# Staging the attention keys: copies by VectorE into three tiles, for transfers into two

## The chip, the cores and the metric

The kernel runs on one core of a Trainium2 chip. The core has five engines that work side by side, each through its own queue in order: TensorE (PE, matmuls and transposes into PSUM), VectorE (DVE), ScalarE (ACT), GpSimd (POOL) and SyncE (SP), which here only issues transfers. The metric is the time of one execution in microseconds on the device. The time before is a median over three runs.

## The reference

Two layers of a transformer trunk work on 512 latent tokens (a grid of 8 rows by 64 columns) and 256 context tokens, with 1024 channels. Each layer normalizes and modulates its input, projects it with one matrix into keys, values, queries and gates, and runs two attentions side by side:

```python
qa = _rmsnorm(hs(a_q, NA_HEADS), q_norm_a)
ka = _rmsnorm(hs(a_k, NA_HEADS), k_norm_a)
a_att = _na_latent(qa, ka, va, cka, cva, rpb, rows)
qb = _rope_2d(_rmsnorm(hs(b_q, GQA_Q_HEADS), q_norm_b), pos_row, pos_col)
b_att = _gqa_latent(qb, k_all, v_all)
out_x = _merge(a_att, b_att, a_z, b_z, g_a, g_b, w_o_a, w_o_b, w_out)
x_new = x + gate_x * out_x
```

The first is neighbourhood attention with 8 heads of 64 channels: a latent query sees a window of 8 rows by 16 columns, with a learned bias, and all context keys. The second is grouped-query attention with 8 query heads and 2 key heads over all 768 tokens. In layer 0 the context tokens are updated too, with queries of their own; layer 1 computes only the latent ones.

## The kernel before, in words

Everything is computed in float32 quality on faster number types. A projection splits weights and activations into a high and a low part and adds three products (`mm3`, lines 460 to 462). Weight chunks are loaded by SP (`load_w2`, line 442, tile `raw`), rounded by ScalarE (line 445, `whi`), and VectorE or GpSimd computes the low part (line 447, `wlo`). Attention works on pairs of fp16 numbers, high and low.

Keys after the turn to channels lie in the tile `ka`, 128 rows by (high or low, four head pairs, 768 tokens). The 128 rows hold the two heads of a pair: the even head in rows 0 to 63, the odd one in rows 64 to 127. The query tile `qa` holds, for one head, the high part in that head's own row half and the low part in the other half. So one matmul over 128 rows forms high and low query times the key, provided the head's 64 key rows stand in both row halves. Making that copy is `stage_k`: for one head it writes a tile of 128 x (2, 768) fp16, twice from the same 64 rows. Before, each half is one transfer issued by SP (line 910). For neighbourhood attention the tile is `akt[e]`, one for the even and one for the odd heads (line 1064), so a head can be staged once the scores of the head two before it are read. For the grouped-query keys `stage_k` fills the tile `gk`, during two of the query projections (lines 1173 to 1175), twice a layer.

The heads go through `pipeline` (line 1045): scores of head h, then values of head h - 1, then a share of a list of independent projections (`fill`, for gates and the other branch), whose matmuls stand between those of the heads. The chain of one head's block of 128 queries is: scores on TensorE (lines 918, 919, 1006), bias and row maximum on VectorE (line 1009), exponential on ScalarE (line 1012), reciprocal and scaling (lines 841 to 847), then `turned`: high half on ScalarE (line 888), low half on GpSimd (line 889), and a transposing transfer issued by SP (line 893) into the tile `ht`. Blocks that are not transposed by transfers go through TensorE and lines 858 to 865. The values are lines 1030 to 1040, and `head_out` (lines 878 to 880) puts them in `za`. SP also issues loads of bias (lines 981 and 983), weights, and stores of gates (line 662).

The order on each engine is written into the program beforehand: a planner walks the listed instructions by their place in the program, with a cost model of its own, and gives each engine its fixed queue. Waits are semaphores. A tile made with a tag and a number of buffers is a ring: the next use of a slot waits until the earlier use has been read.

Of the kernel before, what the change touches and what calls it, by code (L numbers as in the profile page):

```python
# [10 lines left out]
F16 = mybir.dt.float16  # L11
# [63 lines left out]
def hybrid_kernel(es: ExitStack, tc, x, ctx, cvec, w_ada, w_ada0, small, gvec, w_in, w_o_a, w_o_b, w_out,  # L75
                  bias_int, bias_edge, rope, ident_d, out):
    nc = tc.nc
    V, S, G, T = nc.vector, nc.scalar, nc.gpsimd, nc.tensor
# [10 lines left out]
    def nm(s):  # L89
        uid[0] += 1  # L90
        return f"{s}_{uid[0]}"
# [536 lines left out]
    def layer(l, hx, nxt, start):  # L628
# [20 lines left out]
        att = {}  # L649
# [94 lines left out]
        kav = pairs("ka")  # L744
# [93 lines left out]
        if True:  # L838
# [65 lines left out]
            def rows(a, half):  # L904
                return a[64 * half:64 * half + 64]

            def stage_k(src, j, e, to):

                for half in range(2):
                    nc.sync.dma_start(rows(to, half), rows(src, e)[:, :, j, :])  # L910

            def q_pair(src, e, j):
                return src[:, e, j, :]
# [10 lines left out]
            def ctx_scores(q, kh, kl, ct, late=True):  # L924

                pss = ps_score()
                for i in range(2):
                    scores(pss, q[:, 512 + 128 * i:640 + 128 * i], kh, kl,
                           [(256 * i, 256, cut(512, 768))])
                mx = sp.tile([128, 2], F32, tag="mx", name=nm("mx"), bufs=8)  # L930
                V.tensor_reduce(mx, pss.rearrange("p (i n) -> p i n", i=2), AX, ALU.max, negate=True)
                dq = gq_dq if late else na_dq[:, l:l + 1]
                V.tensor_scalar(mx, mx, dq, P_LOG if late else 0.0, ALU.mult, ALU.add)
                p = p_tile()
                r = sp.tile([128, 2], F32, tag="r", name=nm("r"), bufs=8)
                for i in range(2):
                    S.activation(p[:, 256 * i:256 * i + 256], pss[:, 256 * i:256 * i + 256], AF.Exp,
                                 bias=mx[:, i:i + 1], scale=dq, accum_out=r[:, i:i + 1])
                if not late:
                    softmax_tail(p, 512, r, mx, [(0, 256), (256, 512)])  # L940
                turned(p, 512, ct.rearrange("p a i k n -> p (a i k) n"), G)
                return ct, r
# [118 lines left out]
                values_of(7, prev)  # L1061
                run(fill, len(fill))

            akt = [att["p"].tile([128, 2, 768], F16, name=nm("kk"), bufs=1) for _ in range(2)]

            def na_first(h):
                j, e = h // 2, h % 2
                kh, kl = akt[e][:, 0], akt[e][:, 1]
                stage_k(kav, j, e, akt[e])
                q = q_pair(qav, e, j)  # L1070
                st = na_scores(h, q, kh, kl)
                if not first:
                    return st, None
                o = 4096 + 1024 * (h % 2)
                ct = turns[:, o:o + 1024].rearrange("p (a i k n) -> p a i k n", a=2, i=2, k=2)
                return st, ctx_scores(q, kh, kl, ct, False)
# [9 lines left out]

            bg = []
            pipeline(fill, 9, na_first, values_of(za, na_values, vsa[:, 1:2], False), bg=bg)


# [77 lines left out]
            for t in range(qt):  # L1168
                tok_proj(w_q, 512, a_hx, t, evac_bq)
                run(bg, 2)  # L1170
                if t == STAGE_T[0]:
                    split_vb()
                if t in STAGE_T:
                    e = STAGE_T.index(t)
                    stage_k(kbv, 0, e, gkt[:, e])
# [69 lines left out]
        with tc.tile_pool(name=f"mrg{l}", bufs=1, reuse_waits="tile") as mp:  # L1245
# [3 lines left out]
            for v in range(nv):  # L1249
                src = gd[l][8 * v:8 * v + 8].rearrange("k p -> (k p)").unsqueeze(0)  # L1250
# [236 lines left out]
    def nxt():  # L1487
        if not hx1:
            hx1.extend([[big("hx") for _ in range(2)] for _ in range(2)])
        return hx1  # L1490
    layer(0, hx0, nxt, start)
    layer(1, hx1, None, None)


# [73 lines left out]
```

## Time and profile before

| | us |
|---|---|
| median of 3 runs | 1138.68 (1135.82 to 1139.03) |
| the profiled execution | 1141.91 |
| its span in the trace | 1140.0 |
| TensorE busy | 1080.4 |
| VectorE busy | 756.2 |
| ScalarE busy | 608.6 |
| GpSimd busy | 451.1 |

The profiled execution is one run recorded by the hardware; its span starts and ends with the first and last recorded instruction. Rows of groups read: line, engine, operation, output and inputs, shapes, count, then total busy us and mean ns of one, then idle time of the engine before them with what ended it. Rows of waits read: who waited for whom, total us, times, longest. Rows of one line or tile have the shortest, median and longest duration in ns. Rows of a timeline begin with start and duration in us. A line like L447 is a line of the program.

### The profile page before, as it was taken

The numbers are of one execution on the slowest core, as the hardware profiler recorded it, in microseconds if no ns is written. First come the engines' busy times: TensorE is split into PE (matmuls) and PEld (weight loads), VectorE is DVE, ScalarE is ACT, GpSimd is POOL, SyncE is SP. The second block draws the span as 40 slices with busy tenths as digits, with TensorE's granted clock in tenths as the row PEclk, the third lists the DMA queues.
The fourth block names the chain that finished last, engine by engine and source line by source line (L and its number), as shares of the span: only waits on it lengthen the run. The fifth ranks groups of instructions, "written<-read, shape, count | busy, mean of one in ns | idle before, by whom it ended". The sixth has DMA issues, their size and how long they took to land. (4 is left out here: it accounts for less than half of the span.)

```text
span 1140.0 us, 16941 instructions
## 1 busy us (share of the span) xinstructions
PE 1080.4 (95%) x5672; PEld 849.9 (75%) x5672; DVE 756.2 (66%) x1627; ACT 608.6 (53%) x1219; POOL 451.1 (40%) x393
## 2 busy tenths in 40 slices
PE   8999999999999999988999999999987899999998
PEld 5688877788988867665888778887765787666677
DVE  4667978765488577666577775576674675677473
ACT  5455368676333567665230264646685435777431
POOL 1054225455154235374322525332243463564530
PEclk8999999999999999989999999999998999999999
DMA  9555346665553488789433533744566445879742
GB/s 360 199 170 177 90 112 146 155 155 133 176 148 132 122 204 181 162 225 238 158 131 100 188 108 114 232 138 130 121 155 168 131 139 161 194 227 224 199 146 79
DMA packets 249711, 186.08 MB, mean 163 GB/s; under 512 B 160924, under 2 KB 215064, under 8 KB 247960
## 3 DMA queue, kind: packets, MB, share of 16 engines
q1 hardware_dynamic: 242144, 170.47, 55.1%
q0 software_dynamic: 2368, 7.87, 2.1%
q10 hardware_dynamic: 5112, 6.66, 1.9%
q8 instruction: 45, 0.74, 0.3%
q14 instruction: 42, 0.34, 0.1%
HBM read 118.86 MB, written 20.47 MB: 122 GB/s over the span
## 5 line engine op out<-in xcount | busy, mean ns | idle before, releaser
L889 POOL TENSOR_TENSOR h<-p,h 128x256 f16<-128x256 f32 (+2 forms) x104 | 108.5, 1051 | 166.0 <-ACT h L888 127.9
L447 POOL TENSOR_TENSOR wlo<-raw,whi 128x512 fp32r<-128x512 f32 x70 | 96.9, 1387 | 134.6 <-ACT whi L445 108.5
L460 PE MATMUL psf<-hx,whi 128*128 128x512 f32 (+1 forms) x360 | 140.6, 391 | 4.4 <-ACT zt L658 2.2
L462 PE MATMUL psf<-hx,wlo 128*128 128x512 f32 (+1 forms) x360 | 137.9, 383 | 0.0
L461 PE MATMUL psf<-hx,whi 128*128 128x512 f32 (+1 forms) x360 | 137.7, 383 | 0.0
L445 ACT CAST whi<-raw 128x512 fp32r<-128x512 f32 x136 | 83.1, 621 | 79.2 <-DMA raw<-in_w_in_dram 48.7
L461 PE MATMUL psx<-wlo,hx 128*128 128x512 f32 (+1 forms) x328 | 120.8, 369 | 1.3 <-DVE wlo L433 1.3
L460 PE MATMUL psx<-whi,hx 128*128 128x512 f32 (+1 forms) x328 | 121.0, 371 | 0.0
L462 PE MATMUL psx<-whi,hx 128*128 128x512 f32 (+1 forms) x328 | 120.5, 368 | 0.0
L433 POOL TENSOR_TENSOR wlo<-raw,whi 128x512 fp32r<-128x512 f32 x40 | 58.9, 1476 | 125.2 <-ACT whi L430 80.2
L430 ACT CAST whi<-raw 128x512 fp32r<-128x512 f32 x88 | 54.1, 625 | 92.6 <-PE psx L462 31.9
L533 POOL TENSOR_TENSOR ss<-ss,ehalf 128x8 f32<-128x8 f32 (+2 forms) x40 | 63.6, 1595 | 93.0 <-DVE ss L530 88.4
L447 DVE TENSOR_TENSOR wlo<-raw,whi 128x512 fp32r<-128x512 f32 x66 | 70.0, 1063 | 42.2 <-ACT whi L445 41.0
L1199 ACT ACTIVATE p<-pss,mx,vb 128x768 f32<-128x768 f32 x64 | 63.5, 993 | 46.8 <-DVE mx L1198 44.2
L888 ACT CAST h<-p 128x256 f16<-128x256 f32 (+2 forms) x136 | 82.0, 618 | 8.4 <-DMA ht<-h 5.9
L1198 DVE CUSTOM_DVE_ANT_0 p<-pss,vb 128x768 f32<-128x768 f32 x64 | 64.1, 1013 | 28.7 <-PE pss L919 23.9
L460 PEld LDWEIGHTS psf<-hx,whi 128*128 128x128 f32 x360 | 69.4, 193 | 17.6 <-ACT zt L658 3.8
L462 PEld LDWEIGHTS psf<-hx,wlo 128*128 128x128 f32 x360 | 69.1, 192 | 12.3
L461 PEld LDWEIGHTS psf<-hx,whi 128*128 128x128 f32 x360 | 69.2, 192 | 11.2
L460 PE MATMUL psx<-hx,whi 128*128 128x256 f32 (+1 forms) x208 | 70.5, 339 | 6.6 <-ACT whi L445 6.6
L461 PEld LDWEIGHTS psx<-wlo,hx 128*128 128x128 f32 x328 | 62.0, 189 | 12.1 <-DVE wlo L433 2.4
L462 PE MATMUL psx<-hx,wlo 128*128 128x256 f32 (+1 forms) x208 | 69.8, 335 | 0.2 <-POOL wlo L447 0.2
(348 smaller groups left out, 2869.4 us busy)
## 6 DMA issues: line engine op xcount, KB each, us to landing
raw<-in_w_in_dram SPq DMA_DIRECT2D x168, 256.0 KB, 3.1
rawb<-in_w_ada_dram SPq DMA_DIRECT2D x48, 256.0 KB, 2.7
raw<-in_w_out_dram SPq DMA_DIRECT2D x32, 256.0 KB, 3.1
kk<-ka SPq DMA_DIRECT2D x32, 192.0 KB, 3.4
tg<-gs SPq DMA_DIRECT2D x4, 1536.0 KB, 8.2
rawx<-in_w_ada_dram SPq DMA_DIRECT2D x4, 1024.0 KB, 8.5
rawy<-in_w_ada_dram SPq DMA_DIRECT2D x4, 1024.0 KB, 11.1
gs<-zt ACTq DMA_DIRECT2D x16, 256.0 KB, 3.2
```

Of the source, the lines that this page charges most:

```text
L430: S.copy(hi[:, :n], raw[:, :n])
L433: e.tensor_tensor(lo[:, :n], raw[:, :n], F(hi[:, :n]), ALU.subtract)
L445: S.copy(hi, raw)
L447: lo_eng(i).tensor_tensor(lo, raw, F(hi), ALU.subtract)
L460: T.matmul(ps, lhs[0], rhs[0], start=first, stop=False)
L461: T.matmul(ps, lhs[0], rhs[1], start=False, stop=False)
L462: T.matmul(ps, lhs[1], rhs[0], start=False, stop=last)
L533: G.tensor_tensor(ss, ss, ehalf[:, :n], ALU.pow)
L888: S.copy(h[:, 0], p[:, :n])
L889: eng.tensor_tensor(h[:, 1], p[:, :n], h[:, 0], ALU.subtract)
L1198: V.tensor_tensor_reduce(p, pss, lift, gq_ndq, 3e38, ALU.add, ALU.min, mx[:, 0:1])
L1199: S.activation(p, pss, AF.Exp, bias=mx[:, 0:1], scale=gq_dq, accum_out=r[:, i:i + 1])
```

## The change

`stage_k` issues no transfers any more. VectorE copies the 64 rows of the head into both row halves, one instruction for each half. It is used for the neighbourhood keys (8 heads in each of 2 layers, 32 copies) and for the grouped-query keys (2 key heads in each layer, 8 copies). For the neighbourhood keys, the two fixed tiles are replaced by a ring of three tiles that the heads take in turn.

```diff
             def stage_k(src, j, e, to):
 
                 for half in range(2):
-                    nc.sync.dma_start(rows(to, half), rows(src, e)[:, :, j, :])
+                    V.tensor_copy(rows(to, half), rows(src, e)[:, :, j, :])
...
-            akt = [att["p"].tile([128, 2, 768], F16, name=nm("kk"), bufs=1) for _ in range(2)]
-
             def na_first(h):
                 j, e = h // 2, h % 2
-                kh, kl = akt[e][:, 0], akt[e][:, 1]
-                stage_k(kav, j, e, akt[e])
+                kk = att["p"].tile([128, 2, 768], F16, tag="kk", name=nm("kk"), bufs=3)
+                kh, kl = kk[:, 0], kk[:, 1]
+                stage_k(kav, j, e, kk)
```

## The prediction

> **What bounds the kernel now.** I read the page's first lines, then the table of stretches over the stages that stage keys, then what TensorE waited for in them, then the rows of the moved transfers, and last the timeline around the longest stop.
>
> ```profile
> span 1140.0 us, 16941 instructions
> PE 1080.4 (95%) x5672; PEld 849.9 (75%) x5672; DVE 756.2 (66%) x1627; ACT 608.6 (53%) x1219; POOL 451.1 (40%) x393
> ```
>
> TensorE is busy for 1080.4 of 1140.0 us, so all its idle time is 59.6 us. An edit that leaves the matmuls alone can win only out of that, and loses only by adding to it.
>
> ```profile
> core 0: us, PE busy (x) PEld busy (x) DVE busy (x) ACT busy (x) POOL busy (x), PEclk, DMA share, GB/s
> 140.00:290.00 150.00, 144.69 (x882) 117.98 (x881) 106.74 (x311) 102.80 (x237) 67.99 (x75) 0.99 0.59 141
> 780.00:895.00 115.00, 99.99 (x522) 73.33 (x521) 67.78 (x202) 75.58 (x168) 43.13 (x48) 0.97 0.57 141
> 320.00:380.00 60.00, 59.58 (x301) 49.35 (x300) 42.51 (x83) 22.46 (x44) 26.64 (x18) 1.00 0.45 136
> 905.00:945.00 40.00, 38.93 (x193) 32.02 (x192) 30.75 (x57) 16.55 (x37) 24.97 (x21) 1.00 0.45 130
> ```
>
> The first two stretches are the neighbourhood attention of layer 0 and layer 1, the last two hold the staging of the grouped-query keys. TensorE is idle for 5.3 us in the first and 15.0 us in the second. VectorE is busy 71% and 59% of them. What TensorE waited for in layer 0's stretch (first fence) and in layer 1's (second); columns are total us, times, longest:
>
> ```profile
> PE psv L1030 <- DVE ho L879: 2.3, 1, 2.3
> PE psf L460 <- DVE za L660: 2.2, 1, 2.2
> ```
>
> ```profile
> PE psx L460 <- ACT whi L445: 6.6, 2, 6.1
> PE psv L1030 <- DMA ht<-h: 2.0, 2, 1.6
> PE pst L858 <- ACT p L845: 1.8, 2, 1.4
> PE psv L1030 <- ACT h L888: 1.4, 1, 1.4
> PE psv L1030 <- DVE ho L879: 1.4, 1, 1.4
> ```
>
> Most of these end on the softmax chain (row maximum, exponential, scaling, halves, transpose), which runs through VectorE. The 6.1 us stop is another thing: it waits for weights. Its timeline, SP first, then ScalarE, then TensorE:
>
> ```profile
> 842.34 0.66 SPq L910 DMA_DIRECT2D kk<-ka  x1
> ...
> 845.71 0.64 SPq L910 DMA_DIRECT2D kk<-ka  x1
> ...
> 848.27 14.02 SPq L893 DMA_TRANSPOSE ht<-h  x10
> 862.34 0.57 SPq L662 DMA_DIRECT2D gs<-zt  x1
> 863.01 0.94 SPq L442 DMA_DIRECT2D raw<-in_w_in_dram  x2
> ```
>
> ```profile
> 864.63 0.60 ACT L658 ACTIVATE zt<-psf 128x512 f32<-128x512 f32 x1 [2.35 <-DMA gs<-zt]
> 866.26 1.38 ACT L445 CAST whi<-raw 128x512 fp32r<-128x512 f32 x2 [1.03 <-DMA raw<-in_w_in_dram]
> ```
>
> ```profile
> 866.93 0.79 PE L460 MATMUL psx<-hx,whi 128*128 128x512 f32 x1 [6.15 <-ACT whi L445]
> ```
>
> SP spends 14.02 us on ten transposes, and the store and the weight load behind them leave only then. The key copies are part of the same queue.
>
> **The change part by part.** *Removed: 40 transfers from SP.*
>
> ```profile
> L910 SPq DMA_DIRECT2D kk<-ka x32: 607/644/1689, 144.7 to 866.6; - x32
> L910 SPq DMA_DIRECT2D gk<-kb x8: 497/589/609, 335.3 to 927.2; - x8
>   DMA kk<-ka: 0.9, 2
> DMA to landing us min/median/max: 2.7/3.4/4.5
> ```
>
> SP gets back 32 x 0.644 + 8 x 0.589 = 25.3 us. Almost none of it is on the path: TensorE waited for these transfers 0.9 us in all. What the queue gives back elsewhere is bounded by the rows of layer 1 that hang on SP: the weights' 6.6 and the transposes' 2.0, so with the 0.9 at most 9.5 us, and at least nothing. I take the two issues just ahead of the ten transposes, 0.66 + 0.64 = 1.3 us, because a queue that starts them earlier ends them earlier by no more, and the 0.9: **-2.2 us** (0 to -9.5).
>
> *Added: 40 copies on VectorE,* each 64 rows of 2 x 768 fp16. The trace has no copy from fp16 to fp16. The nearest rows have one input in SBUF:
>
> ```profile
> L375 DVE CAST hx<-half 128x512 fp32r<-128x512 f32 x12 | 5.1, 424 | 12.8 <-ACT half L371 12.8
> L385 DVE TENSOR_SCALAR x<-x,ss 128x512 f32<-128x512 f32 x12 | 5.8, 483 | 7.4 <-POOL ss L388 7.4
> L359 DVE TENSOR_SCALAR y<-xt,ss 128x1024 f32<-128x1024 f32 x6 | 4.5, 746 | 0.5 <-POOL ss L357 0.5
> L847 DVE TENSOR_SCALAR_CACHE_REDUCE p<-p,r 128x512 f32<-128x512 f32 x32 | 23.7, 740 | 0.4
> L847 DVE TENSOR_SCALAR_CACHE_REDUCE p<-p,r 128x256 f32<-128x256 f32 x16 | 7.6, 477 | 0.5
> L447 DVE TENSOR_TENSOR wlo<-raw,whi 128x512 fp32r<-128x512 f32 x66 | 70.0, 1063 | 42.2 <-ACT whi L445 41.0 <-PE psf L462 0.8
> ```
>
> L385 to L359 gives (746 - 483) / 512 = 0.514 ns a word; L375 then has 424 - 263 = 161 ns beside its words. A row of a copy holds 3,072 bytes, 768 words: 161 + 0.514 x 768 = 556 ns. The dear end is one element at a time, by L847 (740 - 477) / 256 = 1.03 ns: 161 + 1.03 x 1536 = 1.74 us. The cheap end is L375 itself, 0.42 us. I take 0.56, since an ordinary copy is nearest to L375, a cast, and not to L847, which also sums. To this comes waiting for GpSimd:
>
> ```profile
> L447 DVE TENSOR_TENSOR wlo<-raw,whi x66: 668/694/3998, 99.2 to 1070.6; 128x512 fp32r<-128x512 f32 x66
> L375 DVE CAST hx<-half x12: 413/427/428, 655.6 to 688.5; 128x512 fp32r<-128x512 f32 x12
> ```
>
> L447 has a median of 0.694 and a mean of 1.063 us: 0.37 us a piece lost when it runs beside GpSimd's own L447. L375 shows no such spread. I take the 0.37, so a copy is **0.93 us**, and 40 make 37.2 us: VectorE goes from 756.2 to 793.4 us.
>
> The Trainium skill, "SBUF — State Buffer", section "Who interferes with whom", says that a VectorE copy in a two-port mode and a GpSimd instruction exclude each other for a whole instruction, whichever starts first. By it the copies lose time as L447 does and also hold GpSimd up; L375 alone, which never spread, would say that neither happens. With the lock the sum below is as it stands; without it the copy is 0.56 us, and the forecast would be about 1139.6.
>
> *What of the copies is on the path.* A head takes two, 1.86 us. They stand in VectorE's queue, whose rows, maxima and low halves they delay. In layer 1 six waits of TensorE end on the softmax chain (2 + 2 + 1 + 1 in the rows above); a copy is in front of ready work about as often as VectorE is busy, 59%: 6 x 1.86 x 0.59 = 6.6 us. In layer 0 there are two, 2 x 1.86 x 0.71 = 2.6 us. Against these 9.2 us stands the ring: a third tile lets copies run a head or two early, in VectorE's idle third. I take half, **+4.6 us** (0 to 14.9, which is all eight waits at the full 1.86).
>
> *Cover.* Elsewhere in these stages the copies are hidden by the fill, the projections for gates and values that keep TensorE at 144.69 of 150 us in layer 0; where it runs out, as at 861 us, every head's pair shows, 1.86 us. The eight grouped-query copies (7.4 us) fall where TensorE is busy for 59.58 of 60 and 38.93 of 40 us: **+0.5 us** (0 to 1.5, its idle time there). The wait for a free ring tile moves from SP to VectorE. Behind it stand the next row maxima, and ScalarE waits for those; but the tile was last read three heads earlier, so I put it at 0 (bound: one head's pair, 1.9).
>
> *GpSimd.* It too is stretched at times:
>
> ```profile
> L889 POOL TENSOR_TENSOR h<-p,h x104: 662/679/2380, 162.5 to 1061.9; 128x256 f16<-128x256 f32 x64, 128x768 f16<-128x768 f32 x32, 128x512 f16<-128x512 f32 x8
> ```
>
> Its longest low half takes 2.38 us. If a copy holds it as VectorE is held in L447, its instructions start late: 16 copies x 0.56 us x its busy share, 45% and 38%, is 4.0 and 3.4 us. Half of layer 1's six waits (the transposes' two and the one for L888's halves) lie on the chain that passes GpSimd; half of 3.4 is **+1.7 us** (0 to 7.4). Where layer 1's stop goes, the late thing is next the transposes of the last head.
>
> *The sum.* -2.2 + 4.6 + 0.5 + 1.7 = +4.6 us on the profiled execution, which took 1141.91 us: 1146.5. The median of the three runs, 1138.68, is 3.2 us below it, so I forecast **1143.3 us**. The planner redraws the order of all engines from new costs; the same code idled TensorE for 5.3 us in one layer and 15.0 in the other, so I allow 5 us either way.
>
> **The rivals.** *SP was the brake (faster).* With its copies gone SP reaches the store and the weights of layer 1 early enough that the 6.15 us stop goes, and the transposes' waits with it. For it: SP's unbroken run from 842 to 864. Against it: only 1.3 us of this run are key copies. It gains the 9.5 us; with 2 us lost to the copies, the time is 1138.7 - 7.5 = 1131.2. It decides once SP comes to the load at 863.0 us by over 5 us earlier, more than the copies cost above.
>
> *Hidden both ways (no change).* The ring lets every copy fall into VectorE's idle time (43.3 and 47.2 us) and SP's relief ends in waits for GpSimd. For it: TensorE's 95%. Against it: VectorE's queue is in order, and its idle time is waiting that a ready copy can't always use. Time 1138.7.
>
> *The copy is dear, or not early (much slower).* At 1.74 + 0.37 us, 16 copies are 33.8 us, and layer 0's VectorE would be busy for 140.5 of 150 us; the ring then gains nothing. All eight waits take 2 x 2.11: 8 x 4.22 x 0.6 = 20 us, less 2.2: 1157. The planner setting each pair right before its head's scores, which would make the third tile idle, ends between this and the forecast. Against both: L375.
>
> **How the numbers follow.** Forecast 0.37; SP as the brake 0.33; hidden 0.16; dear or late 0.14. 0.3% of 1138.68 is 3.4 us, about what a measurement of this kernel can tell from no change. Slower is 0.37 + 0.14 = 0.51, same 0.16, faster 0.33. The forecast's own range is 1139 to 1150: the sum's terms with the planner's 5 us. As the signs are split, the range for all runs from the gain of SP less a little, 1130, to the dear copy's near end, 1155.
>
> **What would show it.** Right: copies of about 0.6 us, often stretched to 1 us or more beside GpSimd; VectorE near 793 us; no key transfer on SP; TensorE's waits in layer 1 on ScalarE's and VectorE's softmax lines longer, its idle time there above 15.0 us. Wrong: layer 1's stop before a weight load gone and its stretch shorter than 115 us (SP was the brake), copies at 1.7 us (dear), or TensorE's idle time growing in stages that stage no keys (the planner).

## The result, and the profile after

The changed kernel takes 1130.07 us in the median (1129.48 to 1131.95, 6 runs) against 1138.86 us for the kernel before (1133.20 to 1141.79, 6 runs): a ratio of 0.9933, 95% interval 0.9908 to 0.9958. It is faster by 0.7%, where I had forecast 0.4% slower. First the page of the changed kernel, its head and engines:

```profile
span 1127.7 us, 16945 instructions
PE 1075.9 (95%) x5672; PEld 844.4 (75%) x5672; DVE 786.4 (70%) x1667; ACT 608.8 (54%) x1219; POOL 453.6 (40%) x393
```

The span is 12.3 us shorter, where the medians differ by 8.8: the profiled execution of the kernel before, 1141.91 us, was slower than its median, and that of the changed kernel, 1129.48, the fastest of its six. TensorE is busy for 4.5 us less with the same 5,672 matmuls, and idle for 51.8 us and not 59.6. VectorE has 30.2 us more. Then what has taken the place of the transfers, from the rows of the key tiles and the groups of VectorE:

```profile
L910 DVE COPY kk<-ka x32: 543/558/1616, 152.1 to 835.8; 64x1536 f16<-64x1536 f16 x32
L910 DVE COPY gk<-kb x8: 543/555/558, 338.1 to 914.1; 64x1536 f16<-64x1536 f16 x8
L910 DVE COPY kk<-ka 64x1536 f16<-64x1536 f16 x32 | 26.8, 839 | 0.6
```

A copy takes 0.558 us in the median, with a mean of 0.839 us among the neighbourhood keys and up to 1.616 us. The timeline shows where they stretch, VectorE's pairs of copies first, then GpSimd beside the first of them:

```profile
805.92 2.11 DVE L910 COPY kk<-ka 64x1536 f16<-64x1536 f16 x2
...
824.68 1.11 DVE L910 COPY kk<-ka 64x1536 f16<-64x1536 f16 x2
```

```profile
806.09 1.52 POOL L447 TENSOR_TENSOR wlo<-raw,whi 128x512 fp32r<-128x512 f32 x1 [2.40 <-ACT whi L445]
```

The pair at 824.68 us, with GpSimd idle until 825.94, takes 1.11 us; the one that meets GpSimd's low half takes 2.11. To see where the time went I measure each layer's stage between two landmarks that both kernels have: the first memset of `bint` and the load of `cosn`, with which the next stage begins. The rows of the kernel before, then of the changed one (the second number of each range is layer 1's):

```profile
L975 DVE MEMSET bint<- x2: 272/272/272, 151.3 to 777.4; 128x256 f32 x2
L1099 SPq DMA_DIRECT2D cosn<-in_rope_dram x2: 342/362/383, 289.3 to 893.6; - x2
```

```profile
L975 DVE MEMSET bint<- x2: 272/272/272, 151.2 to 778.0; 128x256 f32 x2
L1098 SPq DMA_DIRECT2D cosn<-in_rope_dram x2: 384/403/422, 289.9 to 878.4; - x2
```

Up to layer 1's stage nothing is won: it begins 0.6 us later. The stage shrinks from 116.2 to 100.4 us, by 15.8; from there to the end 2.9 us are given back. (The load of `cosn` is issued by SP itself, so its place isn't quite the same in both kernels.) The stretch from landmark to landmark, first before, then after:

```profile
777.40:893.60 116.20, 101.19 (x521) 74.06 (x520) 69.29 (x207) 76.40 (x169) 44.42 (x49) 0.97 0.57 141
```

```profile
778.00:878.40 100.40, 93.88 (x489) 67.59 (x488) 82.31 (x223) 75.94 (x170) 45.28 (x49) 1.00 0.51 128
```

TensorE's idle time in it falls from 15.0 to 6.5 us. 32 matmuls are done later instead, which fits with what is given back. What TensorE still waited for (780 to 895 us, changed kernel):

```profile
PE psv L1030 <- DMA ht<-h: 4.1, 1, 4.1
PE pss L1006 <- DVE mx L1009: 2.1, 3, 0.9
```

The 6.1 us stop before a weight load is gone. A new one of 4.1 us stands at the end, before the last head's values, which wait for its transposes; the granted clock behind it is 0.65 from 878.1 to 882.0 us, which lies past the landmark and belongs to what is given back. The old stop cost more than itself, as the stretches around it in the kernel before show (the number behind POOL's is the granted clock):

```profile
860.00:866.00 6.00, 0.47 (x3) 0.20 (x2) 2.01 (x3) 2.83 (x6) 1.93 (x2) 0.95 0.62 168
866.00:873.00 7.00, 6.07 (x16) 4.78 (x17) 1.86 (x2) 2.48 (x4) 2.56 (x2) 0.55 0.95 259
873.00:880.00 7.00, 7.00 (x35) 5.31 (x34) 3.60 (x11) 3.41 (x7) 2.88 (x2) 1.00 0.51 153
```

The granted clock over the 7 us behind the stop is 0.55, with 16 matmuls where the next 7 us hold 35. TensorE is busy for 6.07 of them; 0.45 of that, some 2.7 us by this estimate, is what the low clock adds to the stop. The Trainium skill, "TensorE: Matmul & The Clock Gate", section "HAM oscillation — how this bites in real kernels", says that idle gaps over about 3.4 us put TensorE's clock back to half; this trace agrees with its 0.55 behind 6.15 us. It doesn't agree with 3.4 us as the least: in the kernel before, TensorE also stands idle for 2.34 us until 219.53 us, and from 220.3 to 223.7 us the granted clock is 0.50.

SP's queue in the changed kernel is not empty at all:

```profile
809.58 1.74 SPq L442 DMA_DIRECT2D raw<-in_w_in_dram  x3
...
837.82 6.41 SPq L893 DMA_TRANSPOSE ht<-h  x5
...
846.08 7.73 SPq L893 DMA_TRANSPOSE ht<-h  x6
853.91 1.18 SPq L983 DMA_DIRECT2D bedg<-b_edge  x2
855.19 7.07 SPq L893 DMA_TRANSPOSE ht<-h  x5
...
866.47 1.60 SPq L442 DMA_DIRECT2D raw<-in_w_in_dram  x3
```

Three runs of transposes, of 6.41, 7.73 and 7.07 us, follow each other with little between them, where before 14.02 us stood without a break. But the weights were fetched earlier (809.58 us), so TensorE waits for none here, and the last head's keys are copied at 835 us, where before their transfers left at 865.9.

### The profile page after: what moved, and what is told of

Its sections match the earlier page's. It is cut to its first block, busy times and chain, and to the rows that moved or that the text cites. A ratio compares the mean times of both kernels' runs of the same rounds, so it can differ in the third digit from the quotient of the medians.

```text
span 1127.7 us, 16945 instructions
## 1 busy us (share of the span) xinstructions
PE 1075.9 (95%) x5672; PEld 844.4 (75%) x5672; DVE 786.4 (70%) x1667; ACT 608.8 (54%) x1219; POOL 453.6 (40%) x393
## 5 line engine op out<-in xcount | busy, mean ns | idle before, releaser
L889 POOL TENSOR_TENSOR h<-p,h 128x256 f16<-128x256 f32 (+2 forms) x104 | 110.4, 1068 | 156.4 <-ACT h L888 128.7
L460 PEld LDWEIGHTS psf<-hx,whi 128*128 128x128 f32 x360 | 68.3, 190 | 19.5 <-DVE za L660 4.7
L462 PEld LDWEIGHTS psx<-whi,hx 128*128 128x128 f32 x328 | 61.9, 189 | 10.1 <-DVE hx L376 0.4
```

Source lines behind the costliest of these rows:

```text
L460: T.matmul(ps, lhs[0], rhs[0], start=first, stop=False)
L462: T.matmul(ps, lhs[1], rhs[0], start=False, stop=last)
L889: eng.tensor_tensor(h[:, 1], p[:, :n], h[:, 0], ALU.subtract)
```

## The experiments

Two numbers tell the kernels apart: how long layer 1's stage takes, and when in it the last head's scores begin (both from the first memset). They are from one traced execution of each kernel. Ratios are to the kernel before, run on the same chip.

| kernel | keys by | stage, us | last head at | ratio (95%) |
|---|---|---|---|---|
| before | SP | 116.2 | 97.6 | 1 |
| e8_turned_before | SP | 114.3 | 97.2 | 1.0003 (0.9985 to 1.0021) |
| e5_layer0 | SP in layer 1 | 114.6 | 97.7 | 1.0011 (0.9997 to 1.0026) |
| e12_tied | VectorE, tied to SP | 116.2 | 99.5 | 1.0011 (0.9994 to 1.0028) |
| e1_ring_dma | SP, ring | 107.6 | 87.0 | 0.9958 (0.9935 to 0.9981) |
| e11_early | SP, ring, a head early | 108.0 | 83.0 | 0.9953 (0.9929 to 0.9978) |
| e3_act_queue | ScalarE's queue | 109.0 | 80.5 | 0.9950 (0.9930 to 0.9970) |
| e13_pool_queue | GpSimd's queue | 103.9 | 79.6 | 0.9967 (0.9955 to 0.9980) |
| e15_pool_early | GpSimd's queue, ring, early | 101.9 | 79.0 | 0.9936 (0.9916 to 0.9955) |
| after | VectorE, ring | 100.4 | 72.3 | 0.9933 (0.9908 to 0.9958) |
| e7_turned_after | VectorE, ring | 101.0 | 72.5 | 0.9916 (0.9886 to 0.9946) |
| e4_layer1 | VectorE, ring, in layer 1 | 101.2 | 72.9 | 0.9923 (0.9897 to 0.9948) |
| e2_dve_two | VectorE, two tiles | 102.7 | 76.7 | 0.9897 (0.9871 to 0.9922) |
| e9_sp_dummy | VectorE, two tiles | 102.2 | 79.6 | 0.9915 (0.9887 to 0.9942) |
| e10_sp_tiny | VectorE, two tiles | 99.3 | 76.4 | 0.9857 (0.9828 to 0.9885) |
| e16_tiny64 | VectorE, two tiles | 99.6 | 76.9 | 0.9844 (0.9830 to 0.9859) |
| e14_scratch_copies | VectorE, two tiles | 111.2 | 94.2 | 1.0060 (1.0044 to 1.0076) |
| e6_double | VectorE, ring | 114.0 | 91.5 | 1.0152 (1.0123 to 1.0181) |

Not every row is another order of the work. Compared by operation and tile, the matmuls of layer 1 stand in one order in the kernel before, e8 and e5, and in one order in the changed kernel, e7 and e4; e9, e10 and e16 have one order on all five engines throughout, and e15 differs from e13 only in GpSimd's order and, slightly, in SP's. Rows of one order also tell how well a stage repeats: 114.3 to 116.2 us in the first group, 100.4 to 101.2 in the second.

**Which part, and which layer.** My first theory behind the result was SP's relief: 25 us less to issue. The rivals were the ring and an accident of the planner's order.

e1_ring_dma, the ring with SP's transfers:

```diff
+                kk = att["p"].tile([128, 2, 768], F16, tag="kk", name=nm("kk"), bufs=3)
...
                     nc.sync.dma_start(rows(to, half), rows(src, e)[:, :, j, :])
```

> The ring alone: keys are still copied by transfers on SP, but into the ring of three tiles. Theory SP (the gain of 8.8 us, 1138.9 to 1130.1, is SP's relief in layer 1): no gain, 1136 to 1141. Rival ring (the third tile lets heads be staged early): 1130 to 1133. Rival order (the planner's new order is what gains, whatever the cause it was redrawn for): any time in 1130 to 1145, and a layer 1 stretch that differs from 115 us without SP having less to issue.

1134.46 us, between the theories: some of a gain without any relief of SP. e2_dve_two, the copies with the two fixed tiles:

```diff
-                    nc.sync.dma_start(rows(to, half), rows(src, e)[:, :, j, :])
+                    V.tensor_copy(rows(to, half), rows(src, e)[:, :, j, :])
```

> The copies alone: VectorE copies into the two fixed tiles. Theory SP: all of the gain, 1128 to 1133, TensorE's stop before the weight load in layer 1 gone. Rival ring: little of it, 1136 to 1141, with VectorE waiting for tiles to come free. Rival order: any time in 1128 to 1145.

1125.81 us, below every range given: all of the gain is in the copies, and the third tile isn't needed (the two intervals overlap). e3_act_queue, the transfers on ScalarE's queue:

```diff
-                    nc.sync.dma_start(rows(to, half), rows(src, e)[:, :, j, :])
+                    S.dma_start(rows(to, half), rows(src, e)[:, :, j, :])
```

> The same 40 transfers into the two fixed tiles, issued from ScalarE's queue and not SP's: SP is as free as in the change, the data still moves by the transfer engines, and VectorE has no copies. Theory SP: 1127 to 1134, less what ScalarE loses to 40 issues, 25 us of its queue at 0.63 us each. Rival traffic (the 7.9 MB moved less is what gains): 1136 to 1142. Rival order: any.

1131.74 us, about half of e2's gain, with all the data still moved by transfers: this much needs no less traffic. e4_layer1 and e5_layer0 make the change where `l == 1` and where `l == 0`:

> The change (copies and ring) in layer 1 alone, layer 0 as before, both attentions. Theory SP in layer 1: all of the gain, 1128 to 1133, as the trace of the changed kernel has its 15 us there and loses 0.6 us before it. If the gain needs layer 0's shift (an accident of where layer 1 starts): 1136 to 1141.

> The change in layer 0 alone. Theory: no gain, 1135 to 1141, and layer 1's stage as long as before, 114 to 117 us, its last head late. If layer 0's new order helps on its own: below 1134.

1128.34 and 1138.49 us: layer 1 holds the whole gain, and doesn't need layer 0's.

**SP's time, or the tie to SP's queue.** e9_sp_dummy puts SP's 32 transfers of the neighbourhood keys back beside the copies, into tiles that nobody reads, and e10_sp_tiny does so with little data:

```diff
                 stage_k(kav, j, e, akt[e])
+                for half in range(2):
+                    nc.sync.dma_start(rows(akd[e], half), rows(kav, e)[:, :, j, :])
```

> VectorE copies into two fixed tiles, and beside them SP again issues 32 transfers of the neighbourhood keys, of the full size, into two scratch tiles that nobody reads: the queue and the data are back, nothing waits for them to land. Theory SP: the gain goes, 1134 to 1141 against 1125.8 without the scratch transfers. Rival landing (what gains is that a head's keys are there 0.6 us after the copy starts and not 3.4 us after an issue): the time stays at 1124 to 1129. Rival order: any.

> The same with scratch transfers of 32 tokens for 768, 8 KB each: SP's issues are back, the data hardly. Theory SP, if the issue is what costs: as with the full ones, 1133 to 1141. If the moved data are what costs (transposes landing later beside them): 1124 to 1128 here and 1134 to 1141 with the full ones.

1127.27 and 1119.97 us. With 32 of the 40 transfers issued again and as much data moved by them, the gain stays (in another order than e2's). But they don't stand where they stood: nothing waits for them, and they leave early. The scratch tiles' row of e10, whose layer 1 stage begins at 770.1 us:

```profile
L1072 SPq DMA_DIRECT2D kd<-ka x32: 590/607/1432, 151.5 to 787.5; - x32
```

All are out 17 us into the stage (20 us in e9), where the kernel before issued keys until 89 us. So my theory falls for SP's time as such; what the issues cost late in the stage isn't shown by this. With small transfers the kernel is even faster than without any, which I had not expected. Part of that is data: e9 and e10 have one order of all instructions, issues of nearly one length (630 and 607 ns in the median), and differ by 6.6 us in the ratios. In their traces 2.9 us of it lie in layer 1's stage, where the transfer engines are busy for 66% and 56%; the rest isn't placed. e8_turned_before and e7_turned_after swap a head's two halves, to see whether the planner draws another order for the same work:

```diff
-                for half in range(2):
+                for half in (1, 0):
```

> The kernel before with its two key transfers of a head issued in the other order, lower rows last: the same work for every engine. Theory SP: within 3 us of the kernel before. Rival order: the planner draws another order and the time moves by more than 4 us either way.

> The changed kernel with its two copies of a head in the other order: the same work for every engine. Theory SP: within 3 us of the changed kernel's 1130.1. Rival order: it moves by more than 4 us either way.

1136.87 and 1127.83 us: both stay within 3 us of their kernels. But the order on every engine stayed the same, so they say how well a kernel repeats, and nothing about the worth of another order. The new theory: a head can't start before its keys, and keys brought by SP have a place in a queue of transposes of earlier heads. e12_tied tests it with the tiny transfers of e10, now into the tile that the copy then overwrites:

```diff
+                for half in range(2):
+                    nc.sync.dma_start(rows(akt[e], half)[:, :, 0:32], rows(kav, e)[:, :, j, 0:32])
                 stage_k(kav, j, e, akt[e])
```

> VectorE copies into two fixed tiles, and SP issues the 32 transfers of 32 tokens into those same tiles just ahead, so that a copy waits until its transfer has landed; the copies then overwrite it. Same work as with the tiny transfers into scratch tiles (1120.0), with only the tie to SP's queue added. Theory place: the gain goes or most of it, the stage takes 106 to 117 us, 1129 to 1140. Rival order: 1117 to 1126.

1137.97 us. The instructions and bytes are those of e10_sp_tiny, and the ratio goes from 0.9857 to 1.0011, 17.5 us of 1137: adding the tie takes the gain, and more. The timelines say how. SP, last head's first scores and the stop before the weights in e12_tied:

```profile
844.14 15.65 SPq L893 DMA_TRANSPOSE ht<-h  x11
859.85 1.60 SPq L442 DMA_DIRECT2D raw<-in_w_in_dram  x3
861.49 0.66 SPq L1070 DMA_DIRECT2D kk<-ka  x1
```

```profile
863.48 0.80 PE L460 MATMUL psx<-hx,whi 128*128 128x512 f32 x1 [6.57 <-ACT whi L445]
```

```profile
871.09 0.23 PE L918 MATMUL pss<-kk,qa 128*128 128x128 f16 x1
```

and SP and the last head in e10_sp_tiny:

```profile
816.33 1.48 SPq L442 DMA_DIRECT2D raw<-in_w_in_dram  x3
818.15 7.19 SPq L893 DMA_TRANSPOSE ht<-h  x5
...
833.22 1.02 SPq L442 DMA_DIRECT2D raw<-in_w_in_dram  x2
```

```profile
846.54 0.22 PE L918 MATMUL pss<-kk,qa 128*128 128x128 f16 x1
```

Tied, eleven transposes run without a break, and the weights and the last head's keys leave behind them; the stop of 6 us and the late head come back as they were before. Untied, weights and transposes alternate. The tie works through the plan: 431 matmuls of the stage stand ahead of the last head's first scores in e12, as many as in the kernel before, and 377 in e10 (362 in the changed kernel). Whether what counts is a place in SP's queue or also one in VectorE's isn't separated, since in e12 the copies wait in VectorE's queue for these transfers, 3.0 us in this stage. e11_early lists each head's transfers one head earlier:

```diff
+                for g in range(len(kks), min(h + 2, 8)):
+                    kks.append(att["p"].tile([128, 2, 768], F16, tag="kk", name=nm("kk"), bufs=3))
+                    stage_k(kav, g // 2, g % 2, kks[g])
```

> Keys again by transfers on SP, ring of three tiles, but a head's transfers stand in the program one head earlier, so ahead of the previous head's transposes. Theory place (the heads of layer 1 start late since their keys stand behind other heads' transposes in SP's queue; not the queue's length): the last head's scores start some 75 us after the stage's first memset as with VectorE's copies (72 to 80) and not 97.6 or 87.0, the stage takes 98 to 104 us, the time is 1122 to 1130. Rival order (an accident of the plan): the stage takes anything, as likely 107 to 117 us as the transfers had it so far.

1132.53 us: only half of e2's gain, the stage 108.0 us, the last head at 83.0, and all three outside what I expected. The last head's transfers did leave earlier, at 67.6 us into the stage and not at 88.5; so their place in SP's queue isn't all that makes it late. e13_pool_queue and e15_pool_early (the latter with the ring and the early place of e11) issue the transfers from GpSimd's queue:

```diff
-                    nc.sync.dma_start(rows(to, half), rows(src, e)[:, :, j, :])
+                    G.dma_start(rows(to, half), rows(src, e)[:, :, j, :])
```

> The key transfers into the two fixed tiles, issued from GpSimd's queue, in which no transposes stand. Theory place: keys are tied to neither SP nor VectorE; the last head's scores start 72 to 81 us after the stage's first memset, the stage of layer 1 takes 98 to 106 us, 1122 to 1131. If a transfer as such, with its landing, is what ties: as on ScalarE's queue, 107 to 110 us and 1130 to 1135.

> Transfers on GpSimd's queue, the ring of three and each head listed one head early: the best of both by theory, 1118 to 1128, stage of layer 1 96 to 103 us. If the landing ties: 1130 to 1135.

The stage is as expected, its first row that of e13:

```profile
777.80:881.70 103.90, 96.50 (x500) 69.34 (x499) 68.56 (x206) 75.23 (x169) 50.82 (x61) 1.00 0.66 156
```

103.9 and 101.9 us, the last head at 79.6 and 79.0, with transfers that land no sooner than before (3.7 and 3.6 us in the median, 3.4 before). So it isn't a transfer's landing that ties; what these kernels leave out is the place in SP's queue, with the transposes in it. The whole, 1134.30 and 1131.99 us, misses what I gave: layer 0's stage ends 4.4 us later (its load of `cosn` leaves at 293.7 and not at 289.3), with the issues on GpSimd. The Trainium skill, "DMA: Bandwidth & Descriptors", section "Issuing engines are not separate DMA queues", says that issuing from several engines saves only the sequencer's time to start the transfers. Here that is not the whole: with 32 of SP's issues back (e9) nothing was lost, and with another queue (e13) the stage shrank by 12.3 us. What stands ahead in the queue counts too.

**What a copy costs.** e6_double makes each copy of the changed kernel twice; e14_scratch_copies adds 32 copies to e2 that nobody reads:

```diff
-                for half in range(2):
+                for half in (0, 1, 0, 1):
```

```diff
                 stage_k(kav, j, e, akt[e])
+                for half in range(2):
+                    V.tensor_copy(rows(akd[e], half), rows(kav, e)[:, :, j, :])
```

> The changed kernel with every copy made twice: 40 more copies of 0.56 us, 22 us more on VectorE. My prediction's step has copies cost TensorE half of their time times VectorE's busy share, plus GpSimd held up: 4.6 + 0.5 + 1.7 = 6.8 us slower than the changed kernel, 1134 to 1139. If VectorE's idle time takes them: 1127 to 1133.

> VectorE copies into two fixed tiles (1125.8) and 32 more copies into scratch tiles that nobody reads: VectorE's time alone, with nothing waiting. By the doubled copies (25 us for 40) it costs 20 us if VectorE's time is what they took: 1142 to 1149. If it was their standing ahead of the scores: 1126 to 1134.

1155.24 and 1145.88 us. By the ratios 40 more copies cost 24.9 us (1.0152 against 0.9933), 32 that nobody waits for 18.6 us (1.0060 against 0.9897): 0.6 us each, about a copy's own time. e14's groups and its stage:

```profile
L910 DVE COPY kk<-ka 64x1536 f16<-64x1536 f16 x32 | 29.4, 920 | 0.5
L1072 DVE COPY kd<-ka 64x1536 f16<-64x1536 f16 x32 | 20.3, 634 | 0.9
```

```profile
780.50:891.70 111.20, 99.52 (x511) 71.88 (x509) 93.31 (x238) 75.94 (x169) 45.50 (x49) 0.98 0.48 121
```

The 16 more copies lengthen layer 1's stage by 8.5 us, from 102.7, though VectorE is busy for 93.31 of 111.20 us only. What stands out is their place. Nobody waits for them and the planner has them all early: the last starts 19.4 us into the stage. The first 20 us of the stage, e2's and then e14's, with the scratch copies' row and the first head's first scores in e14:

```profile
773.50:793.50 20.00, 20.00 (x95) 15.46 (x94) 17.25 (x38) 12.22 (x26) 7.61 (x7) 1.00 0.38 112
780.50:800.50 20.00, 17.46 (x72) 13.66 (x71) 19.25 (x32) 7.37 (x13) 5.07 (x4) 0.91 0.27 79
L1072 DVE COPY kd<-ka x32: 533/556/1578, 153.0 to 799.9; 64x1536 f16<-64x1536 f16 x32
799.96 0.23 PE L918 MATMUL pss<-kk,qa 128*128 128x128 f16 x1
```

VectorE is busy there for 17.25 of 20 us in e2 and 19.25 in e14, and the first head's scores begin at 19.5 us into the stage, not 10.9. This delay of 8.6 us is the size of the whole loss, which fits copies that are dear since VectorE is nearly full where they stand. The doubled copies also delay the first head, to 19.3 us from 11.6. The first set has no such price over layer 1's stage: 100.4 to 102.7 us with the copies against 101.9 to 103.9 without, on GpSimd's queue. It does at the start, where the first head's scores begin at 10.9 to 11.6 us and not at 8.6 as in the kernel before; the later heads make that up.

**The planner's draw.** e16_tiny64 has scratch transfers of 64 tokens for 32:

> The scratch transfers with 64 tokens for 32: the same instructions in number and kind, the planner's costs nearly the same. If 1120.0 with 32 tokens is a property of the kernel: 1118 to 1122. If it is one draw of the planner's order among many: anywhere in 1119 to 1129.

1120.99 us. The order is e10's on every engine, so this is one draw of the planner measured twice, and whether that draw is luck among many stays open. e10 and e16 are the fastest kernels of this study, 1.4 and 1.6% below the one before. Their order isn't e2's, and with full-size transfers the same order (e9) takes what e2 takes; what in it makes the small ones win I can't say. e2, at 1125.81, is the fastest that does nothing useless.

## Why the prediction was wrong

The step that failed is the first, *Removed*: I gave SP's relief 2.2 us, "because a queue that starts them earlier ends them earlier by no more", with 9.5 us as the most. Layer 1's stage lost 15.8 us in the traces, 12.3 of them net at the end, and the medians 8.8. Three things were missing. I counted the transfers as time on SP, to be taken away from a queue whose order stays; they were a tie, which gave heads and weight loads their places behind other heads' transposes, and without it the order on all engines is another. e9 and e10 show that a kernel with 32 issues early in the stages keeps the gain, e12 that the tie by itself takes 17.5 us from e10's kernel. My bound took the stop as 6.1 us, although the clock after it was there to read, some 2.7 us more. And the sum has no term for the data that the transfers move: by e9 and e10 32 full transfers can cost up to 6.6 us. How these shares add up to the 8.8 us isn't shown.

That TensorE waited only 0.9 us for these transfers was true, and misled: the plan had already put the last head's scores behind 431 matmuls of the stage, where the changed kernel has 362, so nothing was seen to wait for the keys. What showed it was the head's start, 97.6 us into a stage in which the seven others had begun by 72.

*Added.* The price of a copy was right: 556 ns worked out, 558 measured. With waiting for GpSimd I took 0.93 us, and the mean is 0.839; VectorE got 30.2 us and not 37.2. The mechanism by which I took the 0.37 is seen in the pair of 2.11 us beside GpSimd's low half.

*On the path.* The +4.6 us are not to be found at the end: the first head's scores begin 3.0 us later, and yet layer 1's stage is as short with the copies as with transfers on GpSimd's queue. The rule behind it, waits times VectorE's share, was no good either way: the next 32 copies cost 18.6 us and not the 3.7 that it gives by 32 of 40. It takes VectorE's share over a whole stretch, and in e14 the added copies bunch at its start.

*GpSimd.* +1.7 us was too much to see: its 104 low halves of line 889 went from a mean of 1,051 to 1,068 ns, 1.8 us in all, and GpSimd from 451.1 to 453.6 us.

*The grouped-query keys* were not tried alone; their 8 copies ran at 0.555 us without a stretched one.

*The wait for a free ring tile*, put at 0, was right: VectorE stood idle 0.6 us in all before its neighbourhood copies, and two tiles do as well as three.

*The rivals.* "SP was the brake" gave 1131.2 us and is right in direction and place, with the stop gone. Its reason, the time of SP's issues, isn't shown: only 1.3 us of them stood in the run ahead of the weights. The near hit is luck in part, since the transposes' wait, which it also counted as gone, moved to the last head and grew to 4.1 us. "Hidden both ways" is right of layer 0, whose stage takes 138.0 us before and 138.7 after. "Dear, or not early" did not come: the copies took 0.558 us.

Open: why transfers listed a head early and in a ring (e11) leave the stage at 108.0 us with the last head at 83.0, and why the order of e10 and e16 wins 5 to 6 us over e2. By which of the planner's choices the tie orders the loads behind the transposes is argued; shown is that with the tie they stand there and the gain is gone. That nearly every edit here also redraws the plan, and that one draw can differ from another without any tie, remains a rival for a part of each difference.

## What to carry to other kernels

Before costing a transfer by its queue time or by who waits for it, ask what its place in an in-order queue ties together: list when each repeated unit (here a head) begins, and look for one that begins late with nothing seen to wait. Take the tie away or put it back alone, with a transfer too small to matter, to tell it from the time. Read an engine's slack where the new work will stand, and not as a mean over a stage. And before you take two kernels for two draws of a planner, compare their orders: several of the variants here were the same order again.

## What was not expected of the hardware

A stop of TensorE for 6.15 us was followed by 7 us with a granted clock of 0.55, by the estimate above some 2.7 us on top of the stop. TensorE's total busy time doesn't show this well: it was 1080.4 us in the kernel before and 1075.0 in e8, with the same order and a stop at the same place. A VectorE that is busy for 77% of a stage (79.13 of 102.70 us, e2) was busy for 86% of its first 20 us, and 16 more copies there cost 8.5 us. And 32 transfers of full size that nobody waits for cost up to 6.6 us against small ones, all instructions in the same order (e9 and e10).
